# A batched matrix product on one core: the first load of y, cut into two transfers of every other partition

## The chip, the cores and the metric

The kernel runs on one core of one Trainium2 chip. The metric is device time in microseconds (us) of one execution. A core has five engines that run side by side: TensorE (PE in the profile; its weight loads are PEld), VectorE (DVE), ScalarE (ACT), GpSimd (POOL) and SyncE (SP; SPq where the profile shows what its queue issues). Sixteen DMA engines move data between the chip's memory and SBUF, the core's memory of 128 partitions.

## The reference

```
batch, dim_i, dim_j, dim_k = 32, 256, 512, 384
x: float32 [32, 256, 512]      y: float32 [32, 512, 384]
out = np.einsum('bij,bjk->bik', x, y)      # float32 [32, 256, 384]
```

Thirty-two independent products of a 256 x 512 matrix with a 512 x 384 matrix.

## The kernel before

The batch is worked through in N = 8 groups of Q = 4 products. Each product owns a quarter of the partitions, PQ = 32 of 128. A group's x lies in SBUF as 128 partitions with R = 8 rows of 512 numbers each, so a partition takes 16,384 contiguous bytes of memory. A group's y lies as 128 partitions with T = 16 rows of 384 numbers each, 24,576 contiguous bytes to a partition. Both have two buffers (`x_sb`, `y_sb`, used by group number modulo 2). The results of all eight groups have room of their own in `o_sb`, so that no store has to be done before its buffer is used again.

**SyncE** issues every transfer. Ahead of everything it issues y of group 0, x of group 0, x of group 1 and y of group 1 (line 75), without a wait. For groups 2 to 7 (lines 98 to 102) it waits until GpSimd has cast the x that lies in the buffer and issues the next x (`load_x`, line 69), then waits for the first cast of the next group and issues the next y (`load_y`, line 73). After the loads it issues three stores (`store`, lines 93 to 96): groups 0 to 4, groups 5 and 6, and group 7, each after a wait for the engines that make the results. At line 111 it waits until the three stores have landed.

Each load has a semaphore of its own (`s_x[n]`, `s_y[n]`), which stands at 16 when the load is in.

**GpSimd** casts what has come in to float16: y in pieces (`round_y`, lines 130 to 137; four pieces in groups 0, 6 and 7, two pieces in the others), x in two halves (`round_x`, lines 121 to 128). Group 0 goes y first, then x (lines 139 and 140); all others x first, then y. `round_y` waits at line 131 for the load of y, once, before its first piece.

**VectorE** transposes the cast x in blocks of 32 x 32 (line 156) and copies five of the 16 blocks of results of each half out of PSUM (line 165). **TensorE** multiplies: each group has NE = 2 halves, and each half 16 steps t for four products g on four row tiles of the array (lines 231 to 250), in chunks of STEP = 4 steps, each of which waits for a piece of y and a piece of the transposed x (lines 237 and 238). **ScalarE** copies the other eleven blocks of results out of PSUM (line 199).

So the order at the start is: y of group 0 lands, four casts, x of group 0 (in by then), two casts, transposes, products. The second of the two casts of x of group 0 lets SyncE go on to the load of x of group 2.

Of the kernel before, what the change touches and what calls it, by code (L numbers as in the profile page):

```python
# [11 lines left out]
Q = 4  # L12
# [7 lines left out]
def kernel(  # L20
# [6 lines left out]
    nc = tc.nc  # L27
# [7 lines left out]
    T = J // PQ  # L35
# [4 lines left out]
    def sbuf(name, shape, dtype):  # L40
        return nc.alloc_sbuf_tensor(name, shape, dtype).ap()

    x_sb = [sbuf(f"x_sb{i}", [P, R, J], F32) for i in range(2)]
    y_sb = [sbuf(f"y_sb{i}", [P, T, K], F32) for i in range(2)]
# [8 lines left out]
    s_y = [nc.alloc_semaphore(f"s_y{n}") for n in range(N)]  # L53
# [13 lines left out]
    def load_x(n):  # L67
        src = x[n * Q : (n + 1) * Q].rearrange("g (p r) j -> (g p) r j", r=R)
        return nc.sync.dma_start(out=x_sb[n % 2], in_=src).then_inc(s_x[n], 16)

    def load_y(n):
        src = y[n * Q : (n + 1) * Q].rearrange("g (q t) k -> (g q) t k", t=T)
        return nc.sync.dma_start(out=y_sb[n % 2], in_=src).then_inc(s_y[n], 16)

    for ins in (load_y(0), load_x(0), load_x(1), load_y(1)):
        tc.no_tile_sem_insts.add(ins.ins.name)
    tc.close()
    tc.compile()  # L78
# [9 lines left out]
    def chunk_done(n, e, a):  # L88
        return (n * NE + e) * MARKS + (a + 1 if a < NC - 1 else MARKS)
# [25 lines left out]
    def pieces(n):  # L115
        w = 1 if n in (0, N - 2, N - 1) else 2
        return [(a, a + w) for a in range(0, NC, w)]

    po = nc.gpsimd
# [8 lines left out]
            ).then_inc(s_cast, 1)  # L128

    def round_y(n):  # L130
        po.wait_ge(s_y[n], 16)
        for a, b in pieces(n):
            if n:
                po.wait_ge(s_pe, chunk_done(n - 1, NE - 1, b - 1))
            s = slice(a * STEP, b * STEP)
            ins = po.tensor_copy(y_r[:, s], y_sb[n % 2][:, s])  # L136
            ins.then_inc(s_yr, b - a if b < NC else b - a + NC)

    round_y(0)
    round_x(0)  # L140
    for n in range(1, N):
        round_x(n)
        round_y(n)
# [72 lines left out]
    def product(ps, w, m, start, stop, g):  # L216
        return te.add_instruction(  # L217
            mybir.InstMatmult(
                name=nc.get_next_instruction_name(),
                start_tensor_calc=start,  # L220
                stop_tensor_calc=stop,
                tile_size=(PQ, P),
                tile_position=(PQ * g, 0),
                engine=mybir.EngineType.PE,
                ins=[te.lower_ap(m), te.lower_ap(w)],
                outs=[te.lower_ap(ps)],
            )
        )

    xt = xt_sb.bitcast(MM_DT).rearrange("p t (m c) -> p t m c", c=2)  # L230
    with te.Fori(0, N):
        with te.Fori(0, NE) as e:
            take(s_act)
            take(s_dve)
            for t in range(T):
# [3 lines left out]
                for g in range(Q):  # L239
                    s = slice(g * PQ, (g + 1) * PQ)  # L240
                    ins = product(
                        o_ps[:, e * Q + g, :K],
                        xt[s, t // 2, :, t % 2],
                        y_r[s, t],
                        t == 0,
                        t == T - 1,
                        g,
                    )
# [32 lines left out]
```

## Time and profile before

| | |
|---|---|
| time, median of 3 runs | 132.05 us (131.9 to 132.11) |
| time of the profiled execution | 132.13 us |
| span of the profiled execution, first to last instruction | 130.8 us |
| busy share of the span: PE, DVE, ACT, POOL | 47%, 63%, 64%, 57% |
| share of the one DMA queue that SyncE issues on, of 16 engines | 98.1% |
| read from memory, written to memory | 41.94 MB, 12.58 MB |
| granted TensorE clock, mean | 0.823 |

A row of instructions in order of time gives its start in us, its duration in us, its engine, the line of the kernel, the operation, out<-in and a count; in square brackets stands the time for which the engine was idle before it, and what ended that. In a table by stages, each line begins with the stretch in us; its last columns are the granted TensorE clock, the mean busy share of the 16 DMA engines and the rate in GB/s. The lines on transfers give kilobytes of 1024 bytes and the median time from issue to landing. A packet of a transfer is the piece that one DMA engine moves at a time.

### The profile page before, as it was taken

How to read it: one execution, taken by the hardware profiler on the slowest of the kernel's cores; microseconds unless marked ns; L12 is line 12 of the kernel's file. 1: busy time of each engine (PE TensorE's matmuls, PEld its weight loads, DVE VectorE, ACT ScalarE, POOL GpSimd, SP SyncE). 2: the span in 40 equal slices, each digit the busy share in tenths (PEclk: the TensorE clock that was granted, in tenths of full speed). 3: DMA queues.
4: the chain of work that ended last, by engine and by line, in shares of the span. 5: the costliest groups of instructions: out<-in, count | busy, mean ns of one | idle time of the engine just before them, and what ended most of it. 6: DMA issues, size and time to landing. Idle time of an engine off the chain costs nothing. (4 is left out here: it accounts for less than half of the span.)

```text
span 130.8 us, 3199 instructions
## 1 busy us (share of the span) xinstructions
PE 61.4 (47%) x1024; PEld 46.7 (36%) x1024; DVE 82.7 (63%) x144; ACT 84.1 (64%) x178; POOL 74.2 (57%) x42
## 2 busy tenths in 40 slices
PE   0000009910992589089329905980975499100000
PEld 0000009800991566046129604970953236000000
DVE  0000036899379999985997997599999957920000
ACT  0400000599659989993998899399999957994000
POOL 0006991199929965992899459758973970000000
PEclk9999999995589689977986985599599959965555
DMA  5999999999999999999999999999999999999995
GB/s 120 451 396 441 421 431 451 443 408 428 451 413 421 438 443 401 436 436 443 423 458 398 443 408 466 398 418 436 463 398 408 427 438 425 436 428 421 425 440 248
DMA packets 3379, 54.55 MB, mean 417 GB/s; under 512 B 304, under 2 KB 304, under 8 KB 304
## 3 DMA queue, kind: packets, MB, share of 16 engines
q1 hardware_dynamic: 3376, 54.53, 98.1%
q14 instruction: 3, 0.02, 0.0%
HBM read 41.94 MB, written 12.58 MB: 417 GB/s over the span
## 5 line engine op out<-in xcount | busy, mean ns | idle before, releaser
L165 ACT COPY o_sb<-o_ps (+1 forms) x176 | 82.6, 469 | 31.7 <-PE o_ps L217 29.6
L217 PE MATMUL o_ps<-y_r,xt_sb 32*128 32x384 f16 x1024 | 61.4, 384 | 50.4 <-PEq L214 49.5
L217 PEld LDWEIGHTS o_ps<-y_r,xt_sb 32*128 32x128 f16 x1024 | 46.7, 107 | 64.6 <-issue 56.8
L156 DVE STREAM_TRANSPOSE xt_sb<-x_r 128x256 f32<-128x256 f32 x64 | 38.1, 626 | 30.9 <-POOL x_r L126 18.4
L136 POOL CAST y_r<-y_sb 128x1536 f16<-128x1536 f32 (+1 forms) x22 | 44.3, 2049 | 15.8 <-DMA y_sb<-in_y_dram 15.3
L165 DVE COPY o_sb<-o_ps 32x384 f32 (+1 forms) x80 | 44.6, 557 | 1.6
L126 POOL CAST x_r<-x_sb 128x2048 f16<-128x2048 f32 x16 | 30.2, 1893 | 16.8 <-DVE o_sb L165 12.1
L202 ACT ACT_TABLE_LOAD x1 | 1.3, 1283 | 3.4 <-PEq L78 3.4
L265 POOL MEMSET const-float32-0.0<- 128x1 f32 x1 | 0.1, 98 | 0.2 <-issue 0.2
L202 ACT COPY spare<-const-float32-0.0 1x1 f32<-1x1 f32 x1 | 0.2, 190 | 0.0
L265 POOL MEMSET const-bfloat16-1.0<- 128x1 bf16 x1 | 0.1, 101 | 0.0
L265 POOL MEMSET const-uint8-127<- 128x1 uint8 x1 | 0.1, 101 | 0.0
L265 POOL MEMSET const-float32-1.0<- 128x1 f32 x1 | 0.1, 98 | 0.0
## 6 DMA issues: line engine op xcount, KB each, us to landing
y_sb<-in_y_dram SPq DMA_DIRECT2D x8, 3072.0 KB, 16.8
x_sb<-in_x_dram SPq DMA_DIRECT2D x8, 2048.0 KB, 17.0
out_dram<-o_sb SPq DMA_DIRECT2D x1, 7680.0 KB, 33.9
out_dram<-o_sb SPq DMA_DIRECT2D x1, 3072.0 KB, 17.3
out_dram<-o_sb SPq DMA_DIRECT2D x1, 1536.0 KB, 11.5
```

Source lines behind the costliest of these rows:

```text
L126: po.tensor_copy(x_r[:, e], x_sb[n % 2][:, e * H : (e + 1) * H]).then_inc(s_cast, 1)
L136: ins = po.tensor_copy(y_r[:, s], y_sb[n % 2][:, s])
L156: v.transpose(xt_w[:, w], words[:, e, w]).then_inc(s_xt, 1)
L165: ins = copy(o_sb[g * PQ : (g + 1) * PQ, n, e, h], o_ps[h * PQ : (h + 1) * PQ, e * Q + g, :K],)
L202: a_.copy(spare, nc.const_aps.tensor(0.0, [1, 1], F32))
L217: return te.add_instruction(mybir.InstMatmult(name=nc.get_next_instruction_name(), start_tensor_calc=start, stop_tensor_calc=stop, tile_si ...
L265: nc = _bacc.Bacc("TRN2", target_bir_lowering=False, num_devices=1)
```

## The change

The first load, y of group 0, is no longer one transfer of 128 partitions. It comes in two: partitions 0, 2, 4 to 126, and then partitions 1, 3, 5 to 127. SyncE issues both, one after the other, ahead of x of group 0. Both count on the same semaphore, `s_y[0]`, which then stands at 32 when both are in, and GpSimd waits for 32 before it casts y of group 0. All other loads, the stores and the computation stay as they are.

```
-    for ins in (load_y(0), load_x(0), load_x(1), load_y(1)):
+
+    def load_first(eng, r):
+        src = y[0:Q].rearrange("g (q t) k -> (g q) t k", t=T)
+        return eng.dma_start(out=y_sb[0][r::2], in_=src[r::2]).then_inc(s_y[0], 16)
+
+    first = (load_first(nc.sync, 0), load_first(nc.sync, 1))
+    for ins in (*first, load_x(0), load_x(1), load_y(1)):
         tc.no_tile_sem_insts.add(ins.ins.name)
...
     def round_y(n):
-        po.wait_ge(s_y[n], 16)
+        po.wait_ge(s_y[n], 16 if n else 32)
         for a, b in pieces(n):
```

## The prediction

> **What bounds the kernel now.** I read the page first: its strip of 40 slices and the line of the DMA queue.
>
> ```profile
> span 130.8 us, 3199 instructions
> DMA  5999999999999999999999999999999999999995
> ...
> DMA packets 3379, 54.55 MB, mean 417 GB/s; under 512 B 304, under 2 KB 304, under 8 KB 304
> ...
> q1 hardware_dynamic: 3376, 54.53, 98.1%
> ```
>
> The packets of the one queue fill 98.1% of 16 engines' span. No compute engine is near that (the table in the section on the time before). The strip shows no hole between the first slice and the last. The counts also tell how a transfer is cut up. There are 19 transfers (the issue lines below), and 19 x 16 = 304 small packets: one closing packet on each of 16 engines. The other 3376 - 304 = 3072 are 24 blocks of 128: eight y loads, eight x loads and eight groups of output. So one row of one partition is one packet, and a load of y is 128 packets, eight for each engine.
>
> Then I cut the span into stages, to see whether the queue's rate changes.
>
> ```profile
> core 0: us, PE busy (x) PEld busy (x) DVE busy (x) ACT busy (x) POOL busy (x), PEclk, DMA share, GB/s
> ...
> 1.50:4.00 2.50, 0.00 (x0) 0.00 (x0) 0.00 (x0) 0.55 (x1) 0.00 (x0) 1.00 0.98 285
> 4.00:10.40 6.40, 0.00 (x0) 0.00 (x0) 0.00 (x0) 0.92 (x2) 0.00 (x0) 1.00 0.97 416
> ...
> 20.00:100.00 80.00, 52.59 (x895) 42.05 (x886) 68.48 (x120) 66.02 (x141) 59.13 (x29) 0.83 1.00 429
> ...
> 120.00:127.00 7.00, 0.00 (x0) 0.00 (x0) 0.00 (x0) 0.00 (x0) 0.00 (x0) 0.50 0.99 423
> ```
>
> The last two columns are the DMA share and the rate. Whether the last stage still holds loads is told by the line that issues y (least, median and most ns, then the first and last start):
>
> ```profile
> L73 SPq DMA_DIRECT2D y_sb<-in_y_dram x8: 327/328/531, 0.7 to 84.1; - x8
> ...
> DMA to landing us min/median/max: 10.1/16.8/25.8
> ```
>
> The last load goes out at 84.1 and is in by 84.1 + 25.8 = 109.9 at the latest. So mostly loads move at 429 GB/s, and the stretch from 120 us, which holds nothing but stores, moves at 423. The ceiling is the same for reading and for writing memory, so it lies on what both have in common: the 16 engines and their ways into and out of SBUF. Before 4 us the rate is 285, so 2.50 x (1 - 285 / 429) = 0.84 us are lost at the start, and the stream is as if it had run at full rate from 1.50 + 0.84 = 2.34 us. From there 54.53 MB at 429 GB/s take 127.1 us and end at 129.4 of 130.8. The sum closes: **the time is a start, 127 us of bytes, and an end of 1.4 us.**
>
> Do the waits of SyncE ever leave the queue empty? I read its instructions in order, then its waits.
>
> ```profile
> 0.74 0.39 SPq L73 DMA_DIRECT2D y_sb<-in_y_dram  x1
> 1.18 0.90 SPq L69 DMA_DIRECT2D x_sb<-in_x_dram  x2
> 2.12 0.53 SPq L73 DMA_DIRECT2D y_sb<-in_y_dram  x1
> ...
> 10.87 5.69 POOL L136 CAST y_r<-y_sb 128x1536 f16<-128x1536 f32 x4 [10.43 <-DMA y_sb<-in_y_dram]
> 16.51 3.73 POOL L126 CAST x_r<-x_sb 128x2048 f16<-128x2048 f32 x2
> ...
> 20.27 0.33 SPq L69 DMA_DIRECT2D x_sb<-in_x_dram  x1
> ```
>
> A y load is 3072 KB = 3.146 MB, or 3.146 / 0.429 = 7.33 us at the full rate; an x load is 2.097 MB, or 4.89 us. Y of group 0 is in at about 10.9 us, when GpSimd starts. The three transfers behind it keep the queue full until about 10.9 + 4.9 + 4.9 + 7.3 = 28.0 us. The load issued at 20.27 therefore comes 7.7 us before the queue would run dry: SyncE is not the bound.
>
> At the end:
>
> ```profile
> SPq L111 <- SPq L111: 11.1, 1, 11.1
> ...
> out_dram<-o_sb SPq DMA_DIRECT2D x1, 7680.0 KB, 33.9
> out_dram<-o_sb SPq DMA_DIRECT2D x1, 3072.0 KB, 17.3
> out_dram<-o_sb SPq DMA_DIRECT2D x1, 1536.0 KB, 11.5
> ```
>
> The last store carries 1536 KB, 1.573 / 0.429 = 3.7 us of work, yet lands 11.5 us after its issue: 7.8 us go into waiting behind other bytes and closing. Compute may be several microseconds later without moving the end; bytes may not. Whatever the change does, it does through the queue.
>
> **The change part by part.**
>
> *The second issue.* SyncE's issue of y is done twice, so what stands behind it (x 0, x 1, y 1) is issued later by one issue: 0.39 us by the first row, 0.45 by the next (0.90 for two). None of these may start before y of group 0 is through its rings, which takes until about 10 us, and the second half, issued by about 1.6 us, is needed only when the first half's four packets per engine have gone (3.67 us of bytes). Cost: nothing, under cover of those bytes; without it, 0.45 us.
>
> *The closing packets.* There are 20 transfers in place of 19, so 320 closing packets, one more per engine. Their price has no row of its own. It is above nothing and at most that of an average packet, 130.8 x 0.981 x 16 / 3376 = 0.61 us. The packet holds a few bytes against 16 KB on average, so I take 0 and keep 0.6 for the range.
>
> *The wait.* GpSimd waits once, for 32 in place of 16. Queued behind it are the eight pieces of work of group 0 (casts of y, then of x), and behind those the transposes, the matmuls and the load at 20.27 us. All of them see the landing of the later half. With the bytes at the same rate that is the landing of today.
>
> *The start.* The first transfer has half the rows. If the 0.84 us lost before 4 us grow with the rows of the first transfer, half of it may go. Against that, issues do not get longer with rows: the store of 7680 KB (five groups, so 640 packets) and the loads of 128 of the row of L73 above stand in one narrow band.
>
> ```profile
> L96 SPq DMA_DIRECT2D out_dram<-o_sb x3: 345/390/403, 85.9 to 119.3; - x3
> ```
>
> Bounds for the start: a gain of 0.84 us, or a loss of 0.45 (a fifth issue in the busy start); I take 0.
>
> *The rate of a transfer of 64 partitions.* This decides. Every transfer in the trace has all 128 partitions, and all run at 416 to 429 GB/s. None has 64, so the price is bounded: at best the same 429, costing nothing; at worst half, costing a further 7.33 us over both halves. The ceiling is a ceiling of 16 parallel ways, since loads and stores share it. A transfer reaches that rate only when its 16 engines use different ways at each moment. In a full transfer eight packets per engine can be dealt so that this holds. With every other partition each engine has four packets, and if it takes four rows that follow each other in the transfer, engine 0 has partitions 0, 2, 4, 6 and each engine covers twice the stretch of SBUF for the same bytes. If two engines thereby meet on one way, half the ways stand idle, in the first half and in the second alike. The nearest row speaks for 429, but it is a row of the other shape; I take half the rate, as the likelier arrangement by a small margin, and keep both ends.
>
> The Trainium skill bears on this in "SBUF — State Buffer", section "Door 1: The DMA port swizzle": four neighbouring partitions, and the four 32 further on, go through one port of 16, and the ports set the bandwidth. Partitions 0 to 6 and 32 to 38 by that map share two ports, so engine 0 and engine 4 would collide. Taken only by the set of ports, though, the map speaks against a loss: the even partitions reach all 16. "DMA: Bandwidth & Descriptors", section "Why a DMA increments its semaphore by 16 and not by 1", has 64 rows spread over 16 engines; neither page tells which of the 64 rows an engine gets. The row at 429 GB/s agrees with the size of the ceiling (435 GB/s there); no run here shows 64 partitions.
>
> *Sum.* 130.8 + 7.33 = 138.1 us of span. The profiled execution took 132.13 us, 1.33 more than its span, so 139.46; the median of the runs is 0.08 below that execution, which gives **139.4 us.** Everything behind y of group 0 moves along, GpSimd's casts too, and nothing later absorbs it, for the queue has no hole.
>
> **The rivals.**
>
> *Same bytes, same rate.* The rows are dealt to the engines by their place in SBUF, all 16 ways are used, and y of group 0 lands within 0.2 us of today. For it: 98.1% of the span is bytes and their number is the same; every row reads 416 or more. Against it: no row has this shape. It gives 132.05 us.
>
> The Trainium skill has this as a rule: "DMA: Bandwidth & Descriptors", section "Rules for kernel authors", says that two transfers to disjoint partition halves serialize on the same 16 engines and are not worth making. By that rule the time stays at 132.05.
>
> *A quicker start* (the other side). Rate as before, and the first bytes flow earlier since the first transfer is set up in half the rows. Place: the 0.84 us lost before 4 us. It decides once setting up scales with rows; half of the loss then goes, 132.05 - 0.42 = 131.6 us, at most 131.2. For it: the rate of 285 in that stage. Against it: issues of 328 to 390 ns whatever the rows.
>
> *A small loss.* Rate as before, but one more issue in the start and one more closing packet per engine are not hidden: 0.45 us, at most 0.45 + 0.61 = 1.06. It gives 132.5 us, at most 133.1. Against it: both lie beside 7.3 us of bytes.
>
> *The change does not do what it says*: the two halves could be joined or dealt unevenly. Dealt to eight of 16 engines in both halves, those eight would carry 16 packets for eight, another 7.33 us; the time is that of the forecast, 139.4, and it is counted there. Joined, it is the same as before.
>
> **How the numbers follow.** Half rate, by shared ways or by uneven dealing: 0.45, with a range of its own of 136.5 to 139.9 (the low end where only some packets collide, the high end with the 0.6 us of closing packets). A quicker start: 0.28. The same: 0.15. A small loss: 0.12. A measurement of this kernel tells about 0.2%, 0.26 us, from no change. Faster by more than that is 0.28, within it 0.15, slower 0.45 + 0.12 = 0.57. The forecast is the likeliest case, not a mean, and the cases lie on both sides; a range for 8 in 10 must reach from the quicker start to half rate: 131.3 to 139.9 us. The middle of it holds little.
>
> **What would show it.** Half rate: the stage from 4 to 10.4 us reads near 215 GB/s, GpSimd's first cast starts near 18.2 us in place of 10.87, the load issued at 20.27 goes out near 27.6, and the stages after read 429 again. Uneven dealing would show the same cast time, with the rate of the first stage fed in part by x. If the cast starts at 10.87 within 0.2 us, the rate of 64 partitions is that of 128 and my main step is wrong; if it starts at 10.0 to 10.6, the start was quicker. A lower share of the queue after 20 us would mean that SyncE's waits bind, and then the step that nothing absorbs or adds is wrong. Packets should number 3392 on the queue, 320 of them under 512 B; otherwise the transfer is cut up in another way than I read.

## The result

The changed kernel takes 132.32 us (median of 13 runs, 132.08 to 132.52), the kernel before 132.06 us (median of 13, 131.9 to 132.18): 1.002 times, 95% interval 1.0012 to 1.0029. That is 0.26 us slower, at the edge of what can be measured. The forecast was 139.4 us, slower by 7.3. Its direction holds; its main step, half the rate for transfers of 64 partitions, does not.

The page of the changed kernel, the lines that answer to those shown first of before:

```profile
span 131.0 us, 3200 instructions
...
DMA packets 3395, 54.55 MB, mean 416 GB/s; under 512 B 320, under 2 KB 320, under 8 KB 320
...
q1 hardware_dynamic: 3392, 54.53, 98.1%
```

The transfer is cut up as predicted: 3392 packets on the queue, 320 of them small, one more closing packet for each engine. The queue is still full for 98.1% of the span.

The same stages of the changed kernel (the last two columns are DMA share and GB/s):

```profile
1.50:4.00 2.50, 0.00 (x0) 0.00 (x0) 0.00 (x0) 0.00 (x0) 0.00 (x0) 1.00 0.99 285
4.00:10.40 6.40, 0.00 (x0) 0.00 (x0) 0.00 (x0) 1.47 (x2) 0.00 (x0) 1.00 0.96 411
...
20.00:100.00 80.00, 52.84 (x887) 43.43 (x891) 68.19 (x120) 65.17 (x139) 59.82 (x29) 0.83 1.01 430
```

From 4 to 10.4 us, while y of group 0 comes in by halves, the rate is 411 GB/s (416 before), not 215. Every other partition loads about as fast as all of them. A finer cut of the start, before and then after, shows what did move:

```profile
1.50:2.00 0.50, 0.00 (x0) 0.00 (x0) 0.00 (x0) 0.00 (x0) 0.00 (x0) 1.00 2.76 590
2.00:2.50 0.50, 0.00 (x0) 0.00 (x0) 0.00 (x0) 0.00 (x0) 0.00 (x0) 1.00 0.34 98
```

```profile
1.50:2.00 0.50, 0.00 (x0) 0.00 (x0) 0.00 (x0) 0.00 (x0) 0.00 (x0) 1.00 0.00 0
2.00:2.50 0.50, 0.00 (x0) 0.00 (x0) 0.00 (x0) 0.00 (x0) 0.00 (x0) 1.00 3.42 786
```

A packet's bytes are counted here where it starts, so these rows tell starts, not rates: before, 12 of the 16 first packets, one for each engine, start between 1.5 and 2.0 us (the first at 1.77); after, none does, and all 16 start between 2.0 and 2.5 (the first at 2.06). SyncE's part in that: its first issue alone, then all issues in order of time, both of the changed kernel, and the row of the line that issues the halves (least, median, most ns):

```profile
0.73 0.55 SPq L78 DMA_DIRECT2D y_sb<-in_y_dram  x1
```

```profile
0.73 1.18 SPq L78 DMA_DIRECT2D y_sb<-in_y_dram  x2
1.97 1.14 SPq L69 DMA_DIRECT2D x_sb<-in_x_dram  x2
3.15 0.45 SPq L73 DMA_DIRECT2D y_sb<-in_y_dram  x1
...
11.62 5.70 POOL L142 CAST y_r<-y_sb 128x1536 f16<-128x1536 f32 x4 [11.18 <-DMA y_sb<-in_y_dram]
```

```profile
L78 SPq DMA_DIRECT2D y_sb<-in_y_dram x2: 549/562/575, 0.7 to 1.3; - x2
```

The first issue takes 0.55 us where it took 0.39, 0.16 longer; the first packet comes 0.29 later. So the longer issue accounts for about half of the delay, and the rest passes between the issue and the first packet. GpSimd starts 0.75 us later. That figure overstates the loss: it goes by the slowest of 16 engines, one of which had a first packet of 2.8 us in this profile. In a second profile of the same kernel the cast starts at 11.22.

How far the whole stream is behind can be worked out from the packets of the trace: each packet's bytes are laid over the end of its time, at the steady speed of one engine (24,576 bytes in 0.91 us), summed up to a given moment, and the difference to before is divided by 431 GB/s.

```
us behind the kernel before, at    4 us   30 us   90 us  110 us
the change                         0.21   0.21    0.21    0.32
the change, second profile         0.26   0.26    0.25    0.30
the kernel before, second profile -0.03  -0.05   -0.04   -0.01
```

The loss is there before 4 us and then stays. The last tenth comes near 98 us, where some packets of the last y take 1.0 to 1.3 us in place of 0.91; what slows them I did not find. Packets of up to 1.27 us stand near there in late_512 and late_1536 below too, whose first load is whole, so they need not belong to the change. The ends agree with the table: the last packet ends at 130.31 and 130.28 us in the two profiles of before, and at 130.59 and 130.69 with the change.

### The profile page after: what moved, and what is told of

Same layout as the page of the kernel before. It is cut to its first block, busy times and chain, and to the rows that moved or that the text cites. A ratio compares the mean times of both kernels' runs of the same rounds, so it can differ in the third digit from the quotient of the medians.

```text
span 131.0 us, 3200 instructions
## 1 busy us (share of the span) xinstructions
PE 60.4 (46%) x1024; PEld 47.5 (36%) x1024; DVE 82.4 (63%) x144; ACT 84.1 (64%) x178; POOL 74.2 (57%) x42
## 3 DMA queue, kind: packets, MB, share of 16 engines
q1 hardware_dynamic: 3392, 54.53, 98.1%
## 5 line engine op out<-in xcount | busy, mean ns | idle before, releaser
L223 PE MATMUL o_ps<-y_r,xt_sb 32*128 32x384 f16 x1024 | 60.4, 379 | 51.9 <-PEq L220 51.8
L223 PEld LDWEIGHTS o_ps<-y_r,xt_sb 32*128 32x128 f16 x1024 | 47.5, 107 | 64.4 <-issue 57.5
```

Of the source, the lines that this page charges most:

```text
L223: return te.add_instruction(mybir.InstMatmult(name=nc.get_next_instruction_name(), start_tensor_calc=start, stop_tensor_calc=stop, tile_si ...
```

## The experiments

Two theories for the 0.26 us. **Start theory:** a first transfer of 64 partitions is issued more slowly, its first bytes flow later, and in a queue without a hole a late start is a late end. **Rival:** splitting a load costs by itself, by closing packets or slower small transfers, wherever it stands. Beside these stood the question why the forecast of half the rate failed. All changes are shown against the kernel before, or against the changed kernel where that is said. Each time stands beside the kernel before in the same batch; the ratio with its interval is not the quotient of the two medians.

| run | us | before | ratio, 95% interval |
|---|---|---|---|
| after_again | 132.26 | 132.02 | 1.0016 (1.0005 to 1.0028) |
| before_again | 131.99 | 132.01 | 0.9996 (0.9987 to 1.0005) |
| split_y1 | 132.05 | 132.02 | 1.0000 (0.9986 to 1.0013) |
| split_rows | 132.11 | 132.02 | 1.0002 (0.9990 to 1.0013) |
| all_y_split | 132.32 | 132.02 | 1.0021 (1.0011 to 1.0031) |
| all_but_first | 132.13 | 132.02 | 1.0007 (0.9995 to 1.0020) |
| half_then_split | 132.11 | 132.09 | 1.0000 (0.9991 to 1.0009) |
| rows_then_split | 132.60 | 132.02 | 1.0038 (1.0017 to 1.0060) |
| late_start | 132.00 | 132.09 | 0.9993 (0.9980 to 1.0007) |
| late_512 | 132.10 | 132.07 | 1.0009 (0.9997 to 1.0020) |
| late_1536 | 132.06 | 132.07 | 0.9997 (0.9987 to 1.0008) |
| late_first | 132.65 | 132.01 | 1.0057 (1.0039 to 1.0075) |
| two_queues | 132.74 | 132.01 | 1.0062 (1.0049 to 1.0075) |
| fourths | 132.36 | 132.02 | 1.0029 (1.0019 to 1.0040) |
| halves | 139.88 | 132.01 | 1.0598 (1.0584 to 1.0612) |
| eighths | 139.67 | 132.09 | 1.0575 (1.0558 to 1.0593) |
| middle | 137.04 | 132.02 | 1.0382 (1.0360 to 1.0405) |
| sixteenths | 151.17 | 132.01 | 1.1462 (1.1447 to 1.1477) |

### The two kernels again

> The changed kernel once more, for a second profile. Start theory: the whole 0.26 us comes from bytes that begin to flow later; the rate from 1.5 to 4 us and the start of the first packets show it again (first packets after 2.0 us, not before 1.8), SyncE's first issue again takes about 0.55 us in place of 0.39, and the time is 132.3 us. Chance theory: the late first packets are scatter of one profile, and the profile may as well look like that of before; the time is 132.3 all the same and the cause lies elsewhere.

> The kernel before once more, for a second profile and the scatter between two copies of one kernel: time ratio 1.000 within 0.001; if the start theory holds, first packets again at about 1.77 us and the first issue at 0.39 us; if those are scatter, they move by 0.2 us or more here too.

Both kernels show their start a second time: first issue 0.55 us and no packet before 2.0 us with the change, 0.39 us and first packets at 1.76 us without it. The late start is no scatter of one profile. Two copies of the kernel before differ by 0.0004, so 0.002 can be told.

### The split moved away from the start, and multiplied

split_y1 splits the fourth load in place of the first (and GpSimd waits for 32 ahead of y of group 1):

```
-    for ins in (load_y(0), load_x(0), load_x(1), load_y(1)):
...
+    def load_first(eng, r):
+        src = y[Q : 2 * Q].rearrange("g (q t) k -> (g q) t k", t=T)
+        return eng.dma_start(out=y_sb[1][r::2], in_=src[r::2]).then_inc(s_y[1], 16)
...
+    for ins in (load_y(0), load_x(0), load_x(1), load_first(nc.sync, 0), load_first(nc.sync, 1)):
```

> Y of group 0 whole again; y of group 1, issued fourth, comes in two transfers of every other partition. Start theory: the extra issue lies beside 20 us of queued bytes and costs nothing; first cast at 10.9 us, time 132.06. Theory that a split costs wherever it stands (closing packets, 64-partition packets a little slower): 132.3.

all_y_split splits every y, all_but_first every y but the first:

```
     def load_y(n):
...
-        return nc.sync.dma_start(out=y_sb[n % 2], in_=src).then_inc(s_y[n], 16)
+        for r in range(2):
+            ins = nc.sync.dma_start(out=y_sb[n % 2][r::2], in_=src[r::2]).then_inc(s_y[n], 16)
...
```

> Every load of y comes in two transfers of every other partition. My forecast (half the rate where 64 partitions are loaded): eight times 7.3 us, 190 us. Start theory: rate of 64 partitions as of 128, the eight extra transfers add only eight closing packets an engine; 132.3 to 132.5 us, and the rate from 20 to 100 us stays at 429 GB/s. Theory that each split costs 0.26 us: 132.06 + 8 x 0.26 = 134.1.

> Every load of y but the first comes in two transfers of every other partition; y of group 0 is whole. Start theory (the loss is the later first byte behind the longer first issue of a 64-partition transfer): first packets before 2.0 us, and the time back at 132.06 although seven loads are split. Theory that splits cost by their closing packets or their rate: 132.3, as with all eight split.

One split away from the start: nothing. Eight splits: 132.32, as much as one split at the start costs. Seven splits without the first: 132.13, not told from before. The rival is out; had each split cost 0.26 us, seven would have cost 1.8, and the interval leaves at most 0.26 for all seven. The rate of 64 strided partitions holds in the long stage too; all_y_split from 20 to 100 us:

```profile
20.00:100.00 80.00, 55.63 (x896) 44.28 (x894) 67.61 (x118) 64.97 (x139) 59.05 (x29) 0.83 1.00 428
```

So the seven extra closing packets per engine weigh too little to measure. The issues do not get cheaper later: the line that issues the halves in all_y_split (least, median, most ns; a whole load of x takes at least 333 in the same kernel):

```profile
L74 SPq DMA_DIRECT2D y_sb<-in_y_dram x16: 471/560/653, 0.7 to 85.1; - x16
```

They are only covered there by the bytes already queued.

### The first load split in another way

split_rows divides y of group 0 by its rows t, so that both transfers have all 128 partitions (shown against the changed kernel):

```
-        ... out=y_sb[0][r::2], in_=src[r::2]
+        ... out=y_sb[0][:, r * 8 : r * 8 + 8], in_=src[:, r * 8 : r * 8 + 8]
```

> Y of group 0 in two transfers again, but each has all 128 partitions and half of the rows t (12,288 bytes a partition). Theory that the 64-partition shape makes the first issue longer: the first issue is back at 0.39 us, first packets at 1.77, time near 132.1. Theory that two issues in the start cost by their number: 132.3. There are 128 packets more, half as long; at 0.01 us of fixed cost for a packet that would be 0.08 us.

132.11, with two issues and 128 more packets. The line that issues them:

```profile
L78 SPq DMA_DIRECT2D y_sb<-in_y_dram x2: 392/406/421, 0.7 to 1.2; - x2
```

So it is not the second issue that costs, but something about a first transfer of 64 partitions: its issue is longer and its first packets come later.

half_then_split and rows_then_split put a whole transfer of eight, or of two, of the 16 rows t ahead and split the rest as the change does (half_then_split, against the changed kernel; GpSimd waits for 48):

```
+        p, t = (slice(0, P), slice(0, 8)) if r is None else (slice(r, P, 2), slice(8, T))
+    first = [load_first(nc.sync, r) for r in (None, 0, 1)]
```

> Y of group 0 in three transfers: the first eight of the 16 rows t on all 128 partitions (3.7 us of bytes, cover enough for what follows), then the other eight rows on every other partition, twice. Start theory: first packets before 2.0 us and 132.06 to 132.15. Theory that the split of y of group 0 costs as such: 132.3 or more.

> Y of group 0 in three transfers: the first two of the 16 rows t on all 128 partitions (3,072 bytes a partition), then the other 14 rows on every other partition, twice. Start theory: the first issue is at 0.39 us again and the first packets start before 2.0 us; the first transfer is 0.9 us of bytes, just enough to cover the second issue of 0.55, so 132.06 to 132.2. Theory that the split of y of group 0 costs as such, wherever its bytes begin: 132.3 or more, with one more issue.

Behind eight whole rows the split is free: 132.11 and a ratio of 1.0000. Behind two rows it is not, against what I expected: 132.6, with wide scatter (132.0 to 133.18). Its first transfer is 0.393 MB, 0.9 us of bytes, which I had called just enough cover. Between 4 and 10.4 us its rate is 405 GB/s (half_then_split: 421), and by the packets it is 0.13 us behind at 30 us. That is a part of the 0.6. The packets say more: of the 128 packets of its split rows, 40 take 0.83 to 1.71 us where 0.80 is the usual time, 0.41 us more for each engine on average, and the last packet of all ends at 130.98, 0.67 us later than before. In half_then_split only 7 of the 168 packets of y of group 0 that start after 5 us are slower than usual. So in rows_then_split the split rows did not keep the full rate; what slows them is open.

### Only the issues made later

GpSimd fills an unused tile, and SyncE waits for that; y of group 0 is whole. In the first three runs the wait came to stand behind the first issue; in late_first the first issue itself waits.

```
+    late = sbuf("late", [P, 512], F32)        # 1, 512 or 1536 elements
+    ins = nc.gpsimd.memset(late, 0.0).then_inc(s_sp, 1)
...
+    nc.sync.wait_ge(s_sp, 1)                  # in the first three runs
...
+        ins.wait_op(s_sp, 1, "sem-ge")        # in late_first instead, on each of the first four loads
```

> The kernel before, with y of group 0 whole; only SyncE waits for one small fill on GpSimd before its first issue, so that everything it issues goes out some 0.2 to 0.4 us later. Start theory: a later first byte moves the end by as much, one for one, since the queue has no hole; 132.06 + the delay seen in the issue, 132.3 to 132.45, with no split at all. Theory that a late start is made up for later, and the loss came from elsewhere: 132.06.

> The kernel before again, y of group 0 whole; the fill on GpSimd for which SyncE waits before its first issue now has 512 elements a partition in place of 1 (the fill of one element ended at 0.83 us and held nothing up). Start theory: whatever the first packets are later than 1.77 us, the end is later by the same, one for one; with a fill of some 0.3 to 0.5 us, 132.3 to 132.6. Theory that a late start is made up for: 132.06.

> The same with a fill of 1536 elements, about three times as long. Start theory: the end moves by the delay of the first packets again, some 0.8 to 1.5 us, 132.9 to 133.6. Theory that a late start is made up for: 132.06.

> The kernel before, y of group 0 whole. In the two runs with a longer fill the wait came to stand behind the first issue, so only x and the second y went out late. Here SyncE's first issue itself waits for the fill of 512 elements (it ends at 1.25 us by the earlier profile), so it goes out at about 1.27 us in place of 0.74, and the rest behind it. Start theory: first packets near 2.3 us, and the end later one for one: 132.06 + 0.53 = 132.6. Theory that a late start is made up for: 132.06.

The first three do not test what their text says: the delay missed the first issue. They test another step, though. In late_1536:

```profile
0.73 1.38 POOL L76 MEMSET late<- 128x1536 f32 x1 [0.29 <-POOLq L269]
0.74 0.39 SPq L73 DMA_DIRECT2D y_sb<-in_y_dram  x1
2.14 0.90 SPq L69 DMA_DIRECT2D x_sb<-in_x_dram  x2
3.08 0.44 SPq L73 DMA_DIRECT2D y_sb<-in_y_dram  x1
```

Everything behind the first issue goes out 0.96 us later (2.14 for 1.18), and the time is 132.06: issues covered by queued bytes cost nothing here. In late_first the first issue goes too:

```profile
0.73 0.52 POOL L76 MEMSET late<- 128x512 f32 x1 [0.29 <-POOLq L269]
1.28 0.39 SPq L73 DMA_DIRECT2D y_sb<-in_y_dram  x1
1.73 0.89 SPq L69 DMA_DIRECT2D x_sb<-in_x_dram  x2
```

It is 0.54 us late (1.28 for 0.74), by the packets the stream is 0.52 us behind at 4 us and 0.51 at 90, and the time is 0.64 us longer (interval 0.51 to 0.99). A late first byte is a late end with no split at all: one for one lies within the interval, at its lower edge. Its first packet comes 1.03 us after the start of the issue, as before (1.77 for an issue at 0.74); with the change it is 1.33.

### Two queues

The second transfer is issued by ScalarE (against the changed kernel):

```
-    first = (load_first(nc.sync, 0), load_first(nc.sync, 1))
+    first = (load_first(nc.sync, 0), load_first(nc.scalar, 1))
```

> As the change, but the second transfer of y of group 0 is issued by ScalarE, at the same time as SyncE issues the first. Start theory: what counts is when the first packets start on each engine, which SyncE's first issue alone sets; 132.3, or a little less if a shorter chain of issues on SyncE helps. If the number of issues on SyncE ahead of the loads were the cost: back to 132.06.

132.74: worse, and a miss. Both issues start together and are as long as in the changed kernel:

```profile
0.73 0.54 SPq L78 DMA_DIRECT2D y_sb<-in_y_dram  x1
0.74 0.58 ACTq L78 DMA_DIRECT2D y_sb<-in_y_dram  x1
```

By the packets the stream is 0.15 us behind at 4 us and 0.57 at 40 us. The second part comes between 30 and 40 us, first here, then in before:

```profile
30.00:40.00 10.00, 5.49 (x74) 5.33 (x78) 6.76 (x13) 6.72 (x15) 8.58 (x4) 0.66 0.99 408
```

```profile
30.00:40.00 10.00, 7.58 (x128) 7.10 (x128) 7.08 (x13) 7.09 (x16) 7.68 (x4) 0.67 1.01 434
```

Packets of the third y take up to 2.0 us there. The one profile of all_y_split has such a stretch at the same place, and it was the longest of that kernel's executions (133.09); the profile of two_queues was the shortest of its five (132.47). So the stretch comes with one queue too, and what makes the median 132.74 is open.

### Which partitions a transfer takes

These change only the partitions in each transfer of y of group 0 (and the count that GpSimd waits for): fourths `r::4` in four transfers, eighths `r::8` in eight, halves `r * 64 : r * 64 + 64` in two, sixteenths `r * 16 : r * 16 + 16` in eight, middle 32 to 95, then 0 to 31, then 96 to 127.

> Y of group 0 in two transfers of neighbouring partitions, 0 to 63 and 64 to 127. If 16 engines share half of the ways into SBUF in each of them: half the rate, first cast near 18 us, time near 139.4. If 64 partitions load at the full rate whatever they are: as the change, 132.3.

> Y of group 0 in eight transfers of 16 neighbouring partitions each, one packet per engine and transfer. If ways into SBUF are shared by place, each transfer reaches only a quarter of them: a quarter of the rate, y of group 0 lands some 22 us later, time near 154. If they are not: the full rate; eight issues of about 0.5 us cost something in the start, 4 us of issues beside 7.3 us of bytes, so 132.3 to 133.3.

> Y of group 0 in four transfers of every fourth partition. If the dealing of strided rows always gives each engine a way of its own: two packets per engine and transfer at the full rate, 411 to 425 GB/s from 4 to 10.4 us, time 132.0 to 132.6 by the start alone. If the full rate of every other partition was a property of that stride only: two engines on a way, near 211 GB/s as with neighbouring halves, time near 139.9.

> Y of group 0 in eight transfers of every eighth partition, 16 partitions each. If four neighbouring partitions share a way and partitions 32 apart share it too, every eighth partition reaches only 8 of 16 ways, though it spans all of SBUF: half the rate, packets of 1.9 us, near 211 GB/s from 4 to 10.4 us, time near 139.9. If a wide span is enough for the full rate: as with every fourth, 132.4.

> Y of group 0 in three transfers of neighbouring partitions: 32 to 95, 0 to 31, 96 to 127. If what counts is which ways the partitions reach (partitions 32 apart share one, 64 apart do not): the first transfer reaches all 16 and runs at the full rate, 3.7 us, and the other two reach 8 each and take 1.9 us for each of their two packets, 3.8 us each; in all 11.3 us in place of 7.3, time near 136.1. If the loss of neighbouring partitions comes with their number (64 or fewer) alone: all three at half rate, 14.7 us, time near 139.9.

The stage from 4 to 10.4 us in halves, eighths, sixteenths and fourths, one fence each:

```profile
4.00:10.40 6.40, 0.00 (x0) 0.00 (x0) 0.00 (x0) 1.47 (x2) 0.00 (x0) 1.00 1.01 211
```

```profile
4.00:10.40 6.40, 0.00 (x0) 0.00 (x0) 0.00 (x0) 1.47 (x2) 0.00 (x0) 1.00 1.04 219
```

```profile
4.00:10.40 6.40, 0.00 (x0) 0.00 (x0) 0.00 (x0) 1.47 (x2) 0.00 (x0) 1.00 0.97 115
```

```profile
4.00:10.40 6.40, 0.00 (x0) 0.00 (x0) 0.00 (x0) 1.47 (x2) 0.00 (x0) 1.00 0.95 407
```

And middle, while its first transfer runs, and later:

```profile
4.00:7.00 3.00, 0.00 (x0) 0.00 (x0) 0.00 (x0) 1.47 (x2) 0.00 (x0) 1.00 1.20 434
```

```profile
9.00:16.00 7.00, 0.00 (x0) 0.00 (x0) 0.00 (x0) 0.00 (x0) 0.00 (x0) 1.00 0.90 229
```

The DMA share is near 1 in all of them: the engines are busy whether they move much or little, and only the last column tells them apart. In halves 16 packets are under way at once by 3.1 us, and they take 1.9 us in place of 0.91; no engine is left out, they share. The number of partitions does not decide: 64 run at 211 (halves), 411 (the change) and 434 (middle). Neither does the span: every eighth partition spans all of SBUF and runs at 219. What fits all six is a count of ways, if four neighbours share one and partitions 32 apart share one as well: 16 ways for every other, every fourth and 32 to 95; 8 for 0 to 63, every eighth and 0 to 31; 4 for 16 neighbours, at 115 (125 from 4 to 16 us).

"SBUF — State Buffer" of the Trainium skill, section "Door 1: The DMA port swizzle", gives that map, with some 218 GB/s for 8 ports and 109 for 4; the rows read 211 to 229 and 115 to 125, and agree, the last a little above. Its reading by the set of ports, which the prediction put down as speaking against a loss, was right.

The time of middle is 137.04, 0.9 us above the 136.1 that the same count gave; no run here places that difference.

## Why the prediction was wrong, point by point

- *The bound* holds. The queue is full from start to end, and late_first shows that what is lost at its start is lost at the end.
- *The second issue costs nothing.* Right: late_1536 puts later issues off by 0.96 us at no cost.
- *The closing packets, taken at 0 of at most 0.6.* Right: seven more per engine in all_but_first are not told from nothing. The trace has their price after all: each carries 4 bytes and takes 0.009 us.
- *The rate of 64 partitions, "I take half the rate, as the likelier arrangement".* **This step failed.** The mechanism exists and was priced well: with 0 to 63 and 64 to 127 two engines do share a way, and halves costs 7.9 us where 7.33 were worked out. But I let an engine take four strided rows in succession, partitions 0, 2, 4, 6, and took it that engines sharing two ways would meet on one all the time. Measured: 411 GB/s from 4 to 10.4 us, and of the 112 packets of y of group 0 behind the first 16, 110 take 0.91 to 0.94 us, so they do not. The strided transfer reaches all 16 ways, and reach was the better guide than an assumed dealing. How the 64 rows are dealt is still not known, for the packets do not name their engine: the dealing may be another, or engines that share ways may take turns. The slower packets of rows_then_split would fit the second, but nothing here shows it. The nearest row, 429 GB/s, was the better value.
- *The start, taken at 0 between -0.84 and +0.45.* Within the bounds, but not 0: this is most of the measured 0.26 us, 0.21 and 0.26 before 4 us in the two profiles. The bound from above was an issue more in the start; what costs is the first transfer itself, with an issue of 0.55 for 0.39 us and a first packet 0.29 us later. I had concluded from issues of 327 to 403 ns that they do not get longer with rows. They do not get longer with the bytes, but they change with the partitions that are taken, and every row I had was of transfers with all 128. The line of L73 itself has 531 at its most, the fourth issue in the start, so the band was not as narrow as I read it.
- *The rival of a small loss* (132.5, chance 0.12) came nearest. Its place, the start, was right; its causes were not, since one more issue is free in split_rows and closing packets are in all_but_first.
- *The direction* came out as forecast, slower, by luck: what was forecast to cost 7.33 us costs nothing that shows, and a term that was taken at 0 gave the 0.26.
- *The quicker start* fell with the same finding: half the rows made the set-up longer. The packets, 3392 and 320, came as said. The cast, at 11.62 and 11.22 us, fell between the signs that I had named; the rate decided.

No version here beats the kernel before.

## What to carry to other kernels

Where a queue has no hole, look at what delays its first byte, and let the first transfer be the one that is issued fastest; what stood behind enough queued bytes could be split here at no cost that showed (eight whole rows were enough, two were not). Before a load is divided by partitions, count the ways that each part reaches: every other and every fourth partition kept the full rate, neighbouring halves had half of it, and sixteen neighbours little over a quarter. A transfer's DMA share says nothing of that; the rate does.

## What I had not expected of the hardware

- First issues in the start take 0.54 to 0.60 us for 64, 32 or 16 strided partitions and for 64 neighbours, and 0.39 us for all 128, but also for 16 neighbours (sixteenths: 393 to 420 ns). First packets came after 2.0 us (2.06 to 2.13) in the first group and at 1.75 to 1.77 in the second. So it is not the number of rows alone; what it is, no run tells.
- Sixteen engines on four ways took 3.27 us for a packet, 3.6 times 0.91 and not four times, so sixteenths came to 151.17 us where 154 were expected.
- In fourths the packets are only 0.10 us behind at 30 us and 0.18 at 110, and its time is 0.34 longer. The end goes by the slowest of 16 engines, so one profile places only a part of so small a difference.
